# Other places in the SBUF partition for weights and activations of a 3-pass fp32 decoder trunk on one core

## The chip, the cores and the metric

The kernel runs on one NeuronCore of a Trainium2 chip. The metric is the device time of one execution in microseconds; 1004.0 us is the median of the two runs of the kernel before.

## The reference

Two decoder layers work on x of 256 tokens by 1024 features, all in float32. Layer 0 is a SwiGLU feed-forward (inner width 2816, added at half weight), a chunked gMLP mixer (inner width 2048) and a second feed-forward. Layer 1 is a feed-forward, stick-breaking attention (16 query heads on 4 key/value heads) and a feed-forward. Keys and values come from x between the two layers. Every sublayer reads an RMSNorm of x, and a last RMSNorm follows.

```python
def swiglu(h, w_in, w_out):
    gate, up = jnp.split(h @ w_in, 2, axis=-1)
    return (jax.nn.silu(gate) * up) @ w_out
...
x = x + 0.5 * swiglu(rms_norm(x, ffn_norm[i, 0]), ffn_w_in[i, 0], ffn_w_out[i, 0])
h = rms_norm(x, mix_norm[i])
x = x + (chunked_sgu(h, ...) if i < 1 else stick_breaking_attention(h @ b_w_q, k, v) @ b_w_o)
x = x + 0.5 * swiglu(rms_norm(x, ffn_norm[i, 1]), ffn_w_in[i, 1], ffn_w_out[i, 1])
```

## The kernel before, in words

Activations live transposed: features on the 128 partitions, 256 tokens along the partition. Each float32 operand is split into a high part, rounded to the matmul type fp32r, and a low part, the rest. One product is then three matmuls that add into one PSUM bank (`mm3`, lines 148 to 150):

```python
nc.tensor.matmul(o, al, bh, start=first, stop=False, skip_group_check=True)   # 148
nc.tensor.matmul(o, ah, bl, start=False, stop=False, skip_group_check=True)   # 149
nc.tensor.matmul(o, ah, bh, start=False, stop=last, skip_group_check=True)    # 150
```

The operand named second is streamed through the array, the one named first is loaded into it beforehand (the stationary one), by a weight load of 128 columns for each matmul. In the trace's names, `ga<-xnh,wlo` streams xnh and holds wlo.

**Weights** come in 332 units of 128 x 1024 floats. SyncE loads a unit into a `raw` tile (7 buffers, up to 7 units ahead), ScalarE casts it into `whi` (line 81), VectorE subtracts into `wlo` (line 83; 9 buffers each, up to 5 units ahead).

**The six stages that matter here**, in the order of the program, with the letters that the tile names end in:

- a, b, c, d are the four feed-forwards. The projection in (`ffn_in`, which calls `project`) holds weights and streams the activations xnh/xnl, 128 x 256 at a time, into the banks g and u: 11 steps of 96 matmuls. VectorE and ScalarE turn g and u into `hh`/`hl`. The projection out holds weights and streams hh/hl into the y banks (`Residual.add`), 11 steps of 48. In stage d the projection out is turned round (`out_add`): hh/hl is held, and 512 columns of weights are streamed into yo.
- s is the gMLP mixer: `project_rows` holds xnh/xnl and streams weights (bank v), `u_in` holds weights and streams xnh/xnl (bank uu), and the projection out streams hhs/hls (bank ys).
- q is the attention: the projection of q, then the steps z (q against the keys kz), o (weights a0, a1 against the values vd), and the projection out of oT (bank yo, streamed in 256 columns). Keys and values are made from xk just before stage c (banks kT and v).

All of these tiles come from pools which are laid one after the other along the partition, so a tile's byte address is settled by the sizes of what stands before it. In the built program xnh lies at byte 27,168 and xnl at 35,360 (both 32 modulo 128); the whi, wlo and raw buffers start at 75,872, 112,736 and 47,200 in steps of 4,096 (all 96 modulo 128); hh and hl start at 149,600 and 157,792 in steps of 2,048 (96); kz, vd, xk and oT lie at 0. Slices of them start at multiples of 512 bytes, so these remainders hold for every matmul. The instruction order is the program's own, engine by engine; pools set when a buffer is free again.

Of the kernel before, what the change touches and what calls it, by code (L numbers as in the profile page):

```python
# [8 lines left out]
F32 = mybir.dt.float32  # L9
F32R = mybir.dt.float32r  # L10
# [89 lines left out]
def trunk(  # L100
# [160 lines left out]
    xT = act.tile([P, KC, T], F32, name="xT")  # L261
    xnh = act.tile([P, KC, T], F32R, name="xnh")
    xnl = act.tile([P, KC, T], F32R, name="xnl")
    acc = act.tile([P, T], F32, name="acc")
    rT = act.tile([P, 2], F32, name="rT")

    spare = act.tile([P, P + 1 + 2 * (T + 1)], F32, name="spare")
    rb = spare[:, :T]
# [22 lines left out]

    eps = const.tile([P, 1], F32, name="eps")
    nc.vector.memset(eps, RMS_EPS)
# [38 lines left out]
    def load_x(hf):  # L332

        for d in range(hf * 4, hf * 4 + 4):
            ptr = ybank(f"ptr{d}")
            for tt in range(2):
                W.order(
                    nc.tensor.transpose(
                        ptr[:, tt * P : (tt + 1) * P], xin[tt, hf][:, (d % 4) * P : (d % 4 + 1) * P], ident
                    )  # L340
                )
            if d % 2:
                W.order(nc.vector.tensor_copy(xT[:, d, :], ptr[:, :T]))
            else:
                W.order(nc.scalar.copy(xT[:, d, :], ptr[:, :T]))
        for d in range(hf * 4, hf * 4 + 4):
            prepare(d, [(("ffn", 0), xnh, xnl)], False)
# [95 lines left out]

    XN = (xnh, xnl)

    def ffn_in(tag, j, ids, mid={}, by_bank=False):

        banks = [gbank(f"g{tag}_{j}"), gbank(f"u{tag}_{j}")]
        project(banks, ids, XN, mid, by_bank)
        gs = scratch(f"gs{tag}_{j}")  # L450
        us = scratch(f"us{tag}_{j}")
        nc.vector.tensor_mul(pair(gs), pair(banks[0]), bc2(rb))
        nc.scalar.activation(gs, gs, AF.Silu)
        nc.vector.tensor_mul(pair(us), pair(banks[1]), bc2(rb))
        nc.vector.tensor_mul(us, us, gs)
        hh = hp.tile([P, 512], F32R, tag="hh", name=f"hh{tag}_{j}")
        hl = hp.tile([P, 512], F32R, tag="hl", name=f"hl{tag}_{j}")
        split(hh, hl, us)
        return hh, hl
# [57 lines left out]
    def spatial_bias(hf):  # L517
# [16 lines left out]
        plan00,  # L534
        [(("mix", 0), xnh, xnl)],
        {1: lambda: load_x(1), 3: norm.columns, 4: norm.rows},
# [24 lines left out]
    norm = Rms("m0")  # L561
    project_rows(first[0], plan_v[0], XN, {2: norm.columns})
    project_rows(first[1], plan_v[1], XN, {2: norm.rows})
    for j in range(2):
        v_out(j, first[j])
    for j in range(2, 8):
        bank = gbank(f"v{j}")
        project_rows(bank, plan_v[j], XN)
        v_out(j, bank)
# [14 lines left out]
    def u_in(j):  # L584
        bank = gbank(f"uu{j}")
        project([bank], [[i] for i in plan_u["in", j]], XN)
        u = sg.tile([P, 512], F32, tag="u", name=f"usb{j}", bufs=4)
        nc.vector.tensor_mul(pair(u), pair(bank), bc2(rb))
        nc.scalar.activation(u, u, AF.Gelu_apprx_tanh)
        return u  # L590

    def mix(j, u):
# [20 lines left out]
        nc.vector.tensor_mul(s, s, u)  # L613
        hh = hp.tile([P, 512], F32R, tag="hh", name=f"hhs{j}")
        hl = hp.tile([P, 512], F32R, tag="hl", name=f"hls{j}")
        split(hh, hl, s)
# [6 lines left out]
    for kind, j in U_STEPS:  # L623
# [4 lines left out]
        else:  # L628
            h = hs.pop(j)
            for m in range(2):  # L630
# [3 lines left out]
                else:  # L634
                    tail.append((w, chunk(h, m)))
    close(y, tail, 0, 1.0, [(("ffn", 1), xnh, xnl)])
# [12 lines left out]
    norm = Rms("f1")  # L649
    ffn("b", plan01, [(("kv", 0), xkh, xkl), (("ffn", 2), xnh, xnl)], {1: norm.columns, 2: norm.rows})  # L650

# [24 lines left out]

    ffn("c", plan10, [(("mix", 1), xnh, xnl)])
    zscale = [at.tile([P, 2], F32, name=f"zscale{n}") for n in "pn"]
    oT = [at.tile([P, KC, T], F32R, tag=f"big{p}", name=f"oT{p}") for p in "hl"]

    def q_out(j, bank):
        qh = hp.tile([P, 512], F32R, tag="hh", name=f"qh{j}")
        ql = hp.tile([P, 512], F32R, tag="hl", name=f"ql{j}")
        split(qh, ql, bank)
        return qh, ql

    def q_in(j):
        bank = ybank(f"q{j}")
        project([bank], [[i] for i in plan_q[j]], XN)
        return q_out(j, bank)  # L690
# [58 lines left out]
    def values_of(b, a0, a1):  # L749
# [55 lines left out]
    close(y, tail, 0, 1.0, [(("ffn", 3), xnh, xnl)])  # L805
    att.close()
# [105 lines left out]
```

## Time and profile before

| | us |
|---|---|
| runs of the kernel before | 1003.92 and 1004.09, median 1004.0 |
| the profiled execution, its own time | 1004.4 |
| its span in the trace | 1002.7 |
| PE busy in the span | 982.3 (98%) |
| VectorE, ScalarE, GpSimd busy | 645.2, 504.1, 86.5 |

The span runs from the first to the last instruction; 1.7 us of the execution lie around it. A matmul's row gives the time at which it starts and a duration that runs on past the start of the next one, because matmuls are pipelined: the distance from one start to the next (called the pitch below) is what a matmul costs in a stream of them.

### The profile page before, as it was taken

How to read it: one execution, taken by the hardware profiler on the slowest of the kernel's cores; microseconds unless marked ns; L12 is line 12 of the kernel's file. 1: busy time of each engine (PE TensorE's matmuls, PEld its weight loads, DVE VectorE, ACT ScalarE, POOL GpSimd, SP SyncE). 2: the span in 40 equal slices, each digit the busy share in tenths (PEclk: the TensorE clock that was granted, in tenths of full speed). 3: DMA queues.
4: the chain of work that ended last, by engine and by line, in shares of the span. 5: the costliest groups of instructions: out<-in, count | busy, mean ns of one | idle time of the engine just before them, and what ended most of it. 6: DMA issues, size and time to landing. Idle time of an engine off the chain costs nothing.

```text
span 1002.7 us, 19306 instructions
## 1 busy us (share of the span) xinstructions
PE 982.3 (98%) x8042; PEld 963.5 (96%) x8042; DVE 645.2 (64%) x823; ACT 504.1 (50%) x690; POOL 86.5 (9%) x126
## 2 busy tenths in 40 slices
PE   8999999999999999999999999999997899999996
PEld 8999999999999999999999999999997899999996
DVE  6864675675866775656569755555678775565644
ACT  6643434475544564444448444444487674444433
POOL 4000000020000300000003000000046320000002
PEclk9999999999999999999999999999999999999999
DMA  9966565647555455666564866665643346656511
GB/s 304 322 195 190 169 189 188 190 143 222 184 177 175 133 191 188 193 188 193 186 195 146 247 189 191 189 193 186 190 149 92 97 147 191 207 172 203 176 42 43
DMA packets 135208, 179.56 MB, mean 179 GB/s; under 512 B 5624, under 2 KB 119376, under 8 KB 135120
## 3 DMA queue, kind: packets, MB, share of 16 engines
q1 hardware_dynamic: 134768, 177.76, 56.7%
q8 instruction: 63, 1.03, 0.4%
q0 software_dynamic: 192, 0.52, 0.2%
q14 instruction: 25, 0.20, 0.1%
q10 hardware_dynamic: 160, 0.05, 0.0%
HBM read 176.73 MB, written 1.05 MB: 177 GB/s over the span
## 4 chain that ended last, share of the span: by engine, by line
PE 89%; DVE 5%; ACT 2%; issue 1%; DMA 1%; POOL 1%; SPq 0%; ACTq 0%; POOLq 0%; DVEq 0%
PE yo L148 2%; PE yo L150 2%; PE yo L149 2%; PE yb L148 2%; PE yb L150 2%; PE yb L149 2%; PE ud L148 2%; PE ud L150 2%; PE gd L148 2%; PE ud L149 2%; PE gb L148 2%; PE gd L150 2%; PE gd L149 2%; PE ub L148 2%; PE gc L150 2%; PE gb L150 2%
## 5 line engine op out<-in xcount | busy, mean ns | idle before, releaser
L81 ACT CAST whi<-raw 128x1024 fp32r<-128x1024 f32 (+1 forms) x333 | 342.7, 1045 | 391.0 <-issue 205.3
L83 DVE TENSOR_TENSOR wlo<-raw,whi 128x1024 fp32r<-128x1024 f32 (+1 forms) x333 | 402.1, 1225 | 200.9 <-ACT whi L81 200.0
L290 POOL TENSOR_TENSOR acc<-acc,sq 128x256 f32<-128x256 f32 x39 | 33.8, 867 | 387.5 <-ACT sq L289 385.6
L148 PE MATMUL ga<-xnh,wlo 128*128 128x256 f32 x176 | 50.1, 285 | 0.0
L148 PE MATMUL ya<-hha,wlo 128*128 128x256 f32 x176 | 49.9, 284 | 0.2 <-DVE xT L399 0.2
L148 PE MATMUL yc<-hhc,wlo 128*128 128x256 f32 x176 | 49.9, 284 | 0.1
L148 PE MATMUL yb<-hhb,wlo 128*128 128x256 f32 x176 | 49.9, 284 | 0.0
L149 PE MATMUL ga<-xnl,whi 128*128 128x256 f32 x176 | 49.3, 280 | 0.5 <-DVE xnl L277 0.5
L149 PE MATMUL ya<-hla,whi 128*128 128x256 f32 x176 | 49.7, 282 | 0.0
L148 PE MATMUL gd<-xnh,wlo 128*128 128x256 f32 x176 | 49.7, 282 | 0.0
L149 PE MATMUL yb<-hlb,whi 128*128 128x256 f32 x176 | 49.7, 282 | 0.0
L149 PE MATMUL yc<-hlc,whi 128*128 128x256 f32 x176 | 49.7, 282 | 0.0
L150 PE MATMUL yb<-hhb,whi 128*128 128x256 f32 x176 | 49.6, 283 | 0.0
L148 PE MATMUL ua<-xnh,wlo 128*128 128x256 f32 x176 | 49.1, 279 | 0.5 <-DVE wlo L83 0.5
L150 PE MATMUL ya<-hha,whi 128*128 128x256 f32 x176 | 49.4, 283 | 0.0
L150 PE MATMUL gd<-xnh,whi 128*128 128x256 f32 x176 | 49.4, 281 | 0.0
L150 PE MATMUL ud<-xnh,whi 128*128 128x256 f32 x176 | 49.4, 281 | 0.0
L148 PE MATMUL ud<-xnh,wlo 128*128 128x256 f32 x176 | 49.4, 281 | 0.0
L149 PE MATMUL ud<-xnl,whi 128*128 128x256 f32 x176 | 49.4, 281 | 0.0
L149 PE MATMUL gd<-xnl,whi 128*128 128x256 f32 x176 | 49.4, 281 | 0.0
L150 PE MATMUL yc<-hhc,whi 128*128 128x256 f32 x176 | 49.4, 283 | 0.0
L150 PE MATMUL ga<-xnh,whi 128*128 128x256 f32 x176 | 49.1, 279 | 0.0
(289 smaller groups left out, 3353.6 us busy)
## 6 DMA issues: line engine op xcount, KB each, us to landing
raw<-in_ffn_w_in_dram SPq DMA_DIRECT2D x176, 512.0 KB, 4.5
raw<-in_ffn_w_out_dram SPq DMA_DIRECT2D x88, 512.0 KB, 4.3
raw<-in_a_w_in_dram SPq DMA_DIRECT2D x32, 512.0 KB, 4.4
raw<-in_a_w_out_dram SPq DMA_DIRECT2D x16, 512.0 KB, 3.3
raw<-in_b_w_q_dram SPq DMA_DIRECT2D x8, 512.0 KB, 4.5
raw<-in_b_w_o_dram SPq DMA_DIRECT2D x8, 512.0 KB, 4.0
raw<-in_w_kv_dram SPq DMA_DIRECT2D x4, 512.0 KB, 4.0
xin<-in_x_dram SPq DMA_DIRECT2D x4, 256.0 KB, 4.9
```

The costliest lines, as they stand in the source:

```text
L81: ins = nc.scalar.copy(hi[:, cc], raw[:, cc])
L83: ins = nc.vector.tensor_sub(lo[:, cc], raw[:, cc], hi[:, cc].bitcast(F32))
L148: nc.tensor.matmul(o, al, bh, start=first, stop=False, skip_group_check=True)
L149: nc.tensor.matmul(o, ah, bl, start=False, stop=False, skip_group_check=True)
L150: nc.tensor.matmul(o, ah, bh, start=False, stop=last, skip_group_check=True)
L290: nc.gpsimd.tensor_add(acc, acc, s)
```

## The change

No instruction is added, taken away or moved: on each of the five engines the order, the shapes and the waits are those of before. Only byte addresses change, through empty tiles (`gap`), padding, and wider tiles of which a shifted part is used. The scratch for dynamic DMA at the start of the partition shrinks from 16,384 to 8,192 bytes.

```diff
+    def gap(name, size):
+        pool = ctx.enter_context(tc.tile_pool(name=name, bufs=1))
+        pool.tile([P, size // 4], F32, name=f"{name}t")
...
+    gap("gapw", 32)
     rawp = ctx.enter_context(tc.tile_pool(name="rawp", bufs=7))
     hip = ctx.enter_context(tc.tile_pool(name="hip", bufs=9))
     lop = ctx.enter_context(tc.tile_pool(name="lop", bufs=9))
+    gap("gaph", 64)
...
+    SHIFT = {'a': 4, 's': 8, 'b': 12, 'c': 20, 'q': 24, 'd': 28}
+    def hp_tile(dtype, tag, name):
+        tile = hp.tile([P, 512 + 32], dtype, tag=tag, name=name)
+        n = place[0]
+        return tile[:, n : n + 512]
...
-    xnh = act.tile([P, KC, T], F32R, name="xnh")
-    xnl = act.tile([P, KC, T], F32R, name="xnl")
+    xnb = [act.tile([P, KC * T + 32], F32R, name=f"xn{p}") for p in "hl"]
+    def placed(n):
+        return tuple(t[:, n : n + KC * T].rearrange("p (k t) -> p k t", k=KC) for t in xnb)
+    XS = {n: placed(s) for n, s in {'a': 4, 's': 8, 'b': 12, 'c': 20, 'q': 24, 'd': 28}.items()}
...
-        project(banks, ids, XN, mid, by_bank)
+        place[0] = SHIFT[tag]
+        project(banks, ids, XS[tag], mid, by_bank)
...
-        hh = hp.tile([P, 512], F32R, tag="hh", name=f"hh{tag}_{j}")
-        hl = hp.tile([P, 512], F32R, tag="hl", name=f"hl{tag}_{j}")
+        hh = hp_tile(F32R, tag="hh", name=f"hh{tag}_{j}")
+        hl = hp_tile(F32R, tag="hl", name=f"hl{tag}_{j}")
...
+    at.tile([P, 8], F32, name="gapk")
     kz = [at.tile([P, 4, 2, T], F32R, name=f"kz{p}") for p in "hl"]
     vd = [at.tile([P, 2, 4, 2, 64], F32R, name=f"vd{p}") for p in "hl"]
+    at.tile([P, 16], F32, name="gapx")
...
-    nc = _bacc.Bacc("TRN2", target_bir_lowering=False, num_devices=1)
+    nc = _bacc.Bacc("TRN2", target_bir_lowering=False, num_devices=1, dynamic_dma_scratch_size=8192)
```

A shift counts floats, so 4 is 16 bytes. In the built program whi, wlo and raw lie at 64 modulo 128, the wide xn and hp tiles at 0 plus the shift. The table gives the remainders modulo 128 of the streamed and the held operand, and their distance (streamed minus held, modulo 128), for each stage.

| stage, banks | before: streamed, held | distance | after: streamed, held | distance |
|---|---|---|---|---|
| a in (ga, ua), a out (ya) | 32, 96 and 96, 96 | 64 and 0 | 16, 64 | 80 |
| s: v | 96, 32 | 64 | 64, 32 | 32 |
| s: uu, ys | 32, 96 and 96, 96 | 64 and 0 | 32, 64 | 96 |
| b in (gb, ub), b out (yb) | 32, 96 and 96, 96 | 64 and 0 | 48, 64 | 112 |
| keys, values: kT, v | 0, 96 and 96, 0 | 32 and 96 | 0, 64 and 64, 0 | 64 |
| c in (gc, uc), c out (yc) | 32, 96 and 96, 96 | 64 and 0 | 80, 64 | 16 |
| q: projection | 32, 96 | 64 | 96, 64 | 32 |
| q: z; o with a0 | 0, 96; 96, 0 | 32; 96 | 64, 96; 96, 64 | 96; 32 |
| q: yo | 0, 96 | 32 | 0, 64 | 64 |
| d in (gd, ud) | 32, 96 | 64 | 112, 64 | 48 |
| d out (yo, 512 columns) | 96, 96 | 0 | 64, 112 | 80 |

## Rows read from the trace of the kernel before

**Rows 1.** The page: span, part 1 for PE, part 2's granted clock.
```profile
span 1002.7 us, 19306 instructions
...
PE 982.3 (98%) x8042; PEld 963.5 (96%) x8042; DVE 645.2 (64%) x823; ACT 504.1 (50%) x690; POOL 86.5 (9%) x126
...
PEclk9999999999999999999999999999999999999999
```

**Rows 2.** The page, part 4: the chain that ended last, by engine.
```profile
PE 89%; DVE 5%; ACT 2%; issue 1%; DMA 1%; POOL 1%; SPq 0%; ACTq 0%; POOLq 0%; DVEq 0%
```

**Rows 3.** PE's waits: who for whom, us in total, times, longest.
```profile
PE o L149 <- DVE a0l L154: 6.1, 3, 3.5
```

**Rows 4.** Timeline of PE from 692 us: first and 30th row (start, duration, instruction).
```profile
691.78 0.28 PE L148 MATMUL gc<-xnh,wlo 128*128 128x256 f32 x1
...
695.07 0.28 PE L150 MATMUL gc<-xnh,whi 128*128 128x256 f32 x1
```

**Rows 5.** Timeline of PE from 701.55 us: first and 28th row.
```profile
701.37 0.28 PE L148 MATMUL yc<-hhc,wlo 128*128 128x256 f32 x1
...
704.61 0.28 PE L148 MATMUL yc<-hhc,wlo 128*128 128x256 f32 x1
```

**Rows 6.** Timeline of PE from 840 us: first and 30th row.
```profile
839.78 0.28 PE L148 MATMUL gd<-xnh,wlo 128*128 128x256 f32 x1
...
843.20 0.28 PE L150 MATMUL ud<-xnh,whi 128*128 128x256 f32 x1
```

**Rows 7.** Groups of 689.7–699.8, 701.4–705.6, 839–848 us: count | busy us, mean ns | idle.
```profile
L148 PE MATMUL uc<-xnh,wlo 128*128 128x256 f32 x16 | 4.4, 276 | 0.0
...
L149 PE MATMUL yc<-hlc,whi 128*128 128x256 f32 x13 | 3.7, 283 | 0.0
...
L148 PE MATMUL ud<-xnh,wlo 128*128 128x256 f32 x14 | 3.9, 281 | 0.0
```

**Rows 8.** Groups of the whole run, PE, shapes apart: the moved stages.
```profile
L150 PE MATMUL yc<-hhc,whi 128*128 128x256 f32 x176 | 49.4, 283 | 0.0
...
L150 PE MATMUL gd<-xnh,whi 128*128 128x256 f32 x176 | 49.4, 281 | 0.0
...
L150 PE MATMUL ga<-xnh,whi 128*128 128x256 f32 x176 | 49.1, 279 | 0.0
...
L150 PE MATMUL gb<-xnh,whi 128*128 128x256 f32 x176 | 48.7, 277 | 0.0
...
L150 PE MATMUL uc<-xnh,whi 128*128 128x256 f32 x176 | 48.6, 276 | 0.0
...
L149 PE MATMUL ys<-hls,whi 128*128 128x256 f32 x128 | 36.2, 283 | 0.0
...
L149 PE MATMUL v<-wlo,xnh 128*128 128x256 f32 x128 | 35.7, 279 | 0.0
L150 PE MATMUL uu<-xnh,whi 128*128 128x256 f32 x128 | 35.7, 279 | 0.0
...
L149 PE MATMUL yo<-wlo,hhd 128*128 128x512 f32 x82 | 31.9, 389 | 0.0
```

**Rows 9.** The same view: pairs at distances 32 and 96.
```profile
L150 PE MATMUL yo<-oTh,whi 128*128 128x256 f32 x64 | 17.8, 280 | 0.0
...
L149 PE MATMUL v<-wlo,xkh 128*128 128x256 f32 x16 | 4.5, 282 | 0.0
...
L149 PE MATMUL z<-kzl,qh 128*128 128x512 f32 x8 | 3.2, 397 | 0.0
```

**Rows 10.** Busy us (instructions) by engine in stage b: PE, PEld, DVE, ACT, POOL; PEclk.
```profile
345.00:535.00 190.00, 190.00 (x1636) 189.77 (x1635) 118.51 (x147) 92.89 (x124) 9.14 (x12) 1.00 0.59 183
```

**Rows 11.** DMA issues of the keys: KB, us to landing; the first use of kzh.
```profile
kzh<-kzh POOLq DMA_DIRECT2D x2, 128.0 KB, 5.5
...
L666 POOL DMA_DIRECT2D kzh<-kzh x2: 597/680/762, 547.8 to 548.6; - x2
...
L148 PEld LDWEIGHTS z<-kzh,ql x16: 187/188/192, 740.2 to 783.5; 128*128 128x128 f32 x16
```

More of the change, by code (lines that the diff above doesn't have):

```diff
@@ L134, in trunk @@
     py = ctx.enter_context(tc.tile_pool(name="py", bufs=4, space=PSUM))
+    place = [4]
+    SHIFT = {'a': 4, 's': 8, 'b': 12, 'c': 20, 'q': 24, 'd': 28}
     def gbank(name):
@@ L261, in trunk @@
     xT = act.tile([P, KC, T], F32, name="xT")
-    xnh = act.tile([P, KC, T], F32R, name="xnh")
-    xnl = act.tile([P, KC, T], F32R, name="xnl")
+    xnb = [act.tile([P, KC * T + 32], F32R, name=f"xn{p}") for p in "hl"]
+    def placed(n):
+        return tuple(t[:, n : n + KC * T].rearrange("p (k t) -> p k t", k=KC) for t in xnb)
+    XS = {n: placed(s) for n, s in {'a': 4, 's': 8, 'b': 12, 'c': 20, 'q': 24, 'd': 28}.items()}
     acc = act.tile([P, T], F32, name="acc")
     rT = act.tile([P, 2], F32, name="rT")
-    spare = act.tile([P, P + 1 + 2 * (T + 1)], F32, name="spare")
+    spare = act.tile([P, P + 1 + 2 * (T + 1)], F32, name="spare", padded_shape=[P, 672])
     rb = spare[:, :T]
@@ L290, in square @@
             nc.gpsimd.tensor_add(acc, acc, s)
-    eps = const.tile([P, 1], F32, name="eps")
+    eps = const.tile([P, 1], F32, name="eps", padded_shape=[P, 32])
     nc.vector.memset(eps, RMS_EPS)
@@ L346, in load_x @@
         for d in range(hf * 4, hf * 4 + 4):
-            prepare(d, [(("ffn", 0), xnh, xnl)], False)
+            prepare(d, [(("ffn", 0), *XS["a"])], False)
             if d % 2 == 0:
@@ L442, in project_rows @@
                 mid[kh + 1]()
-    XN = (xnh, xnl)
     def ffn_in(tag, j, ids, mid={}, by_bank=False):
         banks = [gbank(f"g{tag}_{j}"), gbank(f"u{tag}_{j}")]
-        project(banks, ids, XN, mid, by_bank)
+        place[0] = SHIFT[tag]
+        project(banks, ids, XS[tag], mid, by_bank)
         gs = scratch(f"gs{tag}_{j}")
@@ L534, in trunk @@
         plan00,
-        [(("mix", 0), xnh, xnl)],
+        [(("mix", 0), *XS["s"])],
         {1: lambda: load_x(1), 3: norm.columns, 4: norm.rows},
@@ L561, in trunk @@
     norm = Rms("m0")
-    project_rows(first[0], plan_v[0], XN, {2: norm.columns})
-    project_rows(first[1], plan_v[1], XN, {2: norm.rows})
+    project_rows(first[0], plan_v[0], XS["s"], {2: norm.columns})
+    project_rows(first[1], plan_v[1], XS["s"], {2: norm.rows})
     for j in range(2):
@@ L567, in trunk @@
         bank = gbank(f"v{j}")
-        project_rows(bank, plan_v[j], XN)
+        project_rows(bank, plan_v[j], XS["s"])
         v_out(j, bank)
@@ L585, in u_in @@
         bank = gbank(f"uu{j}")
-        project([bank], [[i] for i in plan_u["in", j]], XN)
+        project([bank], [[i] for i in plan_u["in", j]], XS["s"])
+        place[0] = SHIFT["s"]
         u = sg.tile([P, 512], F32, tag="u", name=f"usb{j}", bufs=4)
@@ L613, in mix @@
         nc.vector.tensor_mul(s, s, u)
-        hh = hp.tile([P, 512], F32R, tag="hh", name=f"hhs{j}")
-        hl = hp.tile([P, 512], F32R, tag="hl", name=f"hls{j}")
+        hh = hp_tile(F32R, tag="hh", name=f"hhs{j}")
+        hl = hp_tile(F32R, tag="hl", name=f"hls{j}")
         split(hh, hl, s)
@@ L635, in trunk @@
                     tail.append((w, chunk(h, m)))
-    close(y, tail, 0, 1.0, [(("ffn", 1), xnh, xnl)])
+    close(y, tail, 0, 1.0, [(("ffn", 1), *XS["b"])])
     sgu.close()
@@ L649, in trunk @@
     norm = Rms("f1")
-    ffn("b", plan01, [(("kv", 0), xkh, xkl), (("ffn", 2), xnh, xnl)], {1: norm.columns, 2: norm.rows})
+    ffn("b", plan01, [(("kv", 0), xkh, xkl), (("ffn", 2), *XS["c"])], {1: norm.columns, 2: norm.rows})
     XK = (xkh, xkl)
@@ L675, in trunk @@
             split(vd[0][:, tt, :, r, :], vd[1][:, tt, :, r, :], src)
-    ffn("c", plan10, [(("mix", 1), xnh, xnl)])
+    ffn("c", plan10, [(("mix", 1), *XS["q"])])
     zscale = [at.tile([P, 2], F32, name=f"zscale{n}") for n in "pn"]
@@ L681, in q_out @@
     def q_out(j, bank):
-        qh = hp.tile([P, 512], F32R, tag="hh", name=f"qh{j}")
-        ql = hp.tile([P, 512], F32R, tag="hl", name=f"ql{j}")
+        qh = hp_tile(F32R, tag="hh", name=f"qh{j}")
+        ql = hp_tile(F32R, tag="hl", name=f"ql{j}")
         split(qh, ql, bank)
@@ L688, in q_in @@
         bank = ybank(f"q{j}")
-        project([bank], [[i] for i in plan_q[j]], XN)
+        project([bank], [[i] for i in plan_q[j]], XS["q"])
         return q_out(j, bank)
@@ L742, in transposed @@
             nc.tensor.transpose(t1[:, h * P : (h + 1) * P], a[1][:, h, P:], ident)
-        a0 = [hp.tile([P, 512], F32R, tag=f"h{p}", name=f"a0{p}{b}") for p in "hl"]
+        a0 = [hp_tile(F32R, tag=f"h{p}", name=f"a0{p}{b}") for p in "hl"]
         a1 = [hp.tile([P, T], F32R, tag=f"a1{p}", name=f"a1{p}{b}", bufs=2) for p in "hl"]
@@ L764, in values_of @@
         split(oT[0][:, b, :], oT[1][:, b, :], of)
+    place[0] = SHIFT["q"]
     qs, es, aw, at2 = {}, {}, {}, {}
@@ L768, in trunk @@
     first = [ybank(f"q{j}") for j in range(2)]
-    project([first[0]], [[i] for i in plan_q[0]], XN, {2: norm.columns})
-    project([first[1]], [[i] for i in plan_q[1]], XN)
+    project([first[0]], [[i] for i in plan_q[0]], XS["q"], {2: norm.columns})
+    project([first[1]], [[i] for i in plan_q[1]], XS["q"])
     for t, s in zip(zscale, (0.125, -0.125)):
@@ L804, in trunk @@
             att_step(step[0], int(step[1]))
-    close(y, tail, 0, 1.0, [(("ffn", 3), xnh, xnl)])
+    close(y, tail, 0, 1.0, [(("ffn", 3), *XS["d"])])
     att.close()
```

## The prediction

> **What bounds the kernel now.** I read the page's parts 1 and 2 first. PE is busy for 982.3 of 1002.7 us, and the granted clock is full in all 40 slices [rows 1], so neither a slower clock nor idle time explains much. The chain that ended last is PE for 89% [rows 2], and the longest wait of PE for another engine is 6.1 us in total, in the attention [rows 3]. So the time is the number of matmuls times their pitch, and a change of places can only matter through the pitch.
>
> The pitch is read from the timeline. In stage c's projection in, 29 pitches take 695.07 − 691.78 = 3.29 us, which is 113.4 ns each [rows 4]. In the projection out that follows, 27 pitches take 704.61 − 701.37 = 3.24 us, 120.0 ns each [rows 5]. In stage d's projection in, 29 pitches take 843.20 − 839.78 = 3.42 us, 117.9 ns each [rows 6]. Shape, type and clock are the same in all three. The mean durations in the three stretches are 276, 283 and 281 ns [rows 7]; less the pitch, each leaves 163 ns. That gives a ruler for the gapless groups: pitch = mean duration − 163.
>
> With it the whole run reads as follows [rows 8]: a's projection in 116 ns, b's 114, c's 113, d's 118, the mixer's uu and v 116, the projections out 120, and the turned projection out of d 226 ns for 512 columns. What differs between in and out is the distance of streamed and held operand modulo 128: 64 in, 0 out. But place does not settle it alone: c and d have the same places and run at 113 and 118, and a lies between. So distance 64 allows two pitches, which one stage holds for long stretches, and distance 0 gives 120 and nothing else for long. Pairs at other distances are rare: the attention's yo at distance 32 runs at 280 − 163 = 117, the values' v at 96 at 282 − 163 = 119, and z (512 columns, distance 32) at 397 − 163 = 234 against 226 at distance 0 [rows 9].
>
> **The change part by part.** Since no instruction, order or wait changes, each part is a count times a change of pitch. Nothing in the trace shows 16, 48, 80 or 112 as a distance. The bounds are the fastest and the slowest steady pitch of the 256-column rows, 113.4 and 120 ns [rows 4, 5]. Both signs are open: a moved pair may fall into the fast rhythm or into the slow one. I take 117.5 for every moved pair, which lies between the 117 of yo at distance 32 and the slow rhythm of distance 64 at 117.9 [rows 6, 9]; nothing picks one new distance over another, and these are the rows where a pair holds neither extreme. Each feed-forward has 6 groups of 176 matmuls in (1056) and 3 of 176 out (528).
>
> - b in: 1056 × (117.5 − 114) = +3.7 us. The distance goes from 64 to 112, so the fast rhythm goes, as far as I can tell.
> - c in: 1056 × (117.5 − 113.4) = +4.3 us.
> - a in: 1056 × (117.5 − 116) = +1.6 us. d in: 1056 × (117.5 − 118) = −0.5 us.
> - uu, 384 matmuls: +1.5 ns each, +0.6 us. v, 384: the same, +0.6 us.
> - a, b and c out: 1584 × (117.5 − 120) = −4.0 us. ys, 384: −1.0 us. Distance 0 goes everywhere, and 120 with it.
> - d out, 246 matmuls of 512 columns: between the 226 of distance 0 and the 234 of z [rows 8, 9] I take 229, nearer to the row that has this stage's own shape and operands; 246 × 2.5 = +0.6 us.
> - yo of the attention, 192 matmuls, from distance 32 to 64: from 117 to 115.5, the middle of the two pitches of distance 64, −0.3 us.
> - The other pairs of the attention and of keys and values are some 350 matmuls; 3 ns on each would be 1 us, and I leave them at 0.
>
> The sum is +5.6 us, against the profiled execution of 1004.4 us, which stands 0.4 us above the median. On the median that is 1004.0 + 5.6, or 1010.
>
> What else moves with the addresses: VectorE, ScalarE and the DMAs write and read at the new places. In stage b VectorE is busy for 118.51 and ScalarE for 92.89 of 190 us [rows 10], so a third of VectorE's time covers any slower access, up to about 70 us in that stage; above that the weight split of line 83 would come late. With PE faster by 6% at the very most, that cover stays. The smaller DMA scratch serves the DMAs that GpSimd issues; the key copies are such, they land 5.5 us after issue, near 554 us, and PE first loads against kzh at 740.2 us [rows 11]. I cost both at nothing, and they would have to be late by nearly 190 us to cost anything.
>
> **The rivals.**
>
> *All moved pairs fall into the fast rhythm.* In its favour, it is the state in which stages b and c spend most of their time [rows 8], and 113.4 is what a pair reaches when nothing holds it up as far as this trace goes. Against it, none of the pairs at distance 0, 32 or 96 reaches it in the mean, and even distance 64 lost it through the whole of d. Its sum: b −0.6, a −2.7, d −4.9, uu −1.0, v −1.0, the three outs 1584 × −6.6 = −10.5, ys −2.5, d out 246 × −6.6 = −1.6, yo −0.7: −26 us, 978 us.
>
> *The new distances lock at the slow rhythm.* Distance 0 held 120 ns for thousands of matmuls, so a slow rhythm is as stable as the fast one, and v at distance 96 stands at 119 [rows 9]. If every moved pair goes to 120, the projections in pay: b +6.3, c +7.0, a +4.2, d +2.1, uu +1.5, v +1.5, and d out at 234 pays +2.0, yo +0.6, while the outs gain nothing: +25 us, 1029 us. A matmul of 256 columns counts about 7,000 times among the moved pairs, so 1 ns is 7 us. From a mean moved pitch of 119.6 ns on, 2.1 ns above my 117.5, the result is slower by over 2% (20 us), which is about what a measurement of this kernel can tell from no change.
>
> *The places do nothing.* The difference between in and out could come from something other than the place, such as the pattern of PSUM banks. Then every group keeps its pitch, and the time stays at 1004 us. Against it: v streams weights and holds activations, with the places of uu exchanged, and has the pitch of uu, not that of the outs [rows 8]; and z and yo differ from the outs in the direction in which their distances differ [rows 9]. For it: c and d differ at equal places. The Trainium skill, in "SBUF — State Buffer", section "Who interferes with whom", gives PE two independent read ports, one for the streamed operand and one for weight loads, and says that PE never waits for anyone. By that rule no place could cost anything and the sum would be 0; the trace with 113.4 and 120.0 ns for one shape at one clock does not bear it out so far, so this rival keeps a small chance.
>
> **How the numbers follow.** My forecast, a mixture of rhythms about 117.5 ns with stages of both signs, gets 0.70; the fast lock 0.06; the slow lock 0.12; no effect 0.12. Of the six new distances some will lie above 117.5 and some below; if each stage of some 1,500 matmuls is off by 2.5 ns either way, that is 4 us a stage, and about 9 us for six independent ones. The range goes from 990 to 1028, two such steps to either side and rounded outward below, so that it takes in most of the slow lock and leaves out the outer part of the fast one. Faster by over 2% is the fast lock alone, 0.06; slower is the slow lock, 0.12; within 2% is all the rest, 0.82.
>
> **What would show it right or wrong.** The order of instructions stays, so each group of rows 8 can be laid beside its own successor. If I am right, the groups of ya, yb, yc and ys fall from 283 towards 280 ns, those of b and c in rise from 277 and 276 towards 280, and d in stays near 281. Different distances should give different pitches; if all groups stand unchanged, the places do nothing. A stage at a mean of 276 or 283 throughout has locked fast or slow. I would be wrong in kind, not in size, if PE's waits for VectorE or for DMA grew from a few us to tens, if the granted clock fell, or if a group went clearly above 283 or below 276, outside both bounds.

## The result and the profile after

The changed kernel takes 1014.84 us (median of 1014.15 and 1015.53), the kernel before 1004.0. The ratio is 1.0109, 95% interval 1.008 to 1.0139: slower by about 1%. The profiled execution took 1015.53 us.

The page of the changed kernel: span, part 1 for PE, the granted clock, and part 4 by engine.
```profile
span 1013.8 us, 19306 instructions
...
PE 996.1 (98%) x8042; PEld 976.9 (96%) x8042; DVE 643.3 (63%) x823; ACT 503.7 (50%) x690; POOL 85.0 (8%) x126
...
PEclk9999999999999999999999999999999999999999
...
PE 89%; DVE 5%; ACT 2%; issue 1%; POOL 1%; DMA 1%; SPq 0%; ACTq 0%; POOLq 0%; DVEq 0%
```

PE's waits in the changed kernel (us in total, times, longest), the two largest.
```profile
PE o L166 <- DVE a0l L171: 4.6, 2, 3.4
PE o L165 <- DVE a0l L171: 2.4, 1, 2.4
```

The span grew by 11.1 us and PE's busy time by 996.1 − 982.3 = 13.8 us, with the same 8,042 matmuls at the same full clock [rows 1]. The chain is PE for 89% as before [rows 2], the waits in the attention stay at a few us (4.6 + 2.4 in total; the largest total before was 6.1 [rows 3]), and PE's idle time in the span went from 1002.7 − 982.3 = 20.4 to 17.7 us. So the time is not in waits; the matmuls follow one another more slowly. One stretch of stage b shows it: the columns are those of rows 10, PE's instructions stand in its first bracket.
```profile
345.00:535.00 190.00, 190.00 (x1617) 189.69 (x1616) 116.41 (x141) 90.09 (x115) 5.83 (x9) 1.00 0.60 186
```
In the same 190 us without a gap, 1,617 matmuls start where 1,636 did [rows 10]. VectorE and ScalarE have as much room as before.

Groups of the whole run in the changed kernel, shapes apart (count | busy us, mean ns of one | idle); lines 165 to 167 are 148 to 150 of before.
```profile
L167 PE MATMUL gb<-xnh,whi 128*128 128x256 f32 x176 | 50.0, 284 | 0.0
...
L167 PE MATMUL ya<-hha,whi 128*128 128x256 f32 x176 | 49.3, 282 | 0.0
...
L167 PE MATMUL uc<-xnh,whi 128*128 128x256 f32 x176 | 49.3, 280 | 0.0
...
L166 PE MATMUL gb<-xnl,whi 128*128 128x256 f32 x176 | 49.2, 279 | 0.0
...
L167 PE MATMUL gd<-xnh,whi 128*128 128x256 f32 x176 | 49.1, 279 | 0.0
...
L167 PE MATMUL yc<-hhc,whi 128*128 128x256 f32 x176 | 49.0, 280 | 0.0
...
L165 PE MATMUL gb<-xnh,wlo 128*128 128x256 f32 x176 | 49.0, 278 | 0.0
...
L167 PE MATMUL yb<-hhb,whi 128*128 128x256 f32 x176 | 48.6, 277 | 0.0
...
L167 PE MATMUL uu<-xnh,whi 128*128 128x256 f32 x128 | 36.1, 282 | 0.0
...
L166 PE MATMUL v<-wlo,xnh 128*128 128x256 f32 x128 | 36.0, 281 | 0.0
L166 PE MATMUL ys<-hls,whi 128*128 128x256 f32 x128 | 36.0, 281 | 0.0
...
L166 PE MATMUL yo<-wlo,hhd 128*128 128x512 f32 x82 | 32.3, 394 | 0.0
```
Each line against its own successor in rows 8: b and c in rise from 277 and 276 to 284 and 280, uu and v from 279 to 282 and 281, and d out from 389 to 394; d in falls from 281 to 279. The outs part: b falls from 283 to 277, c to 280, ys to 281, a only to 282. The three lines of one product no longer agree (b in: 278, 279 and 284), so a single group's mean is not a measure of its stage here.

From here on the pitch is the mean distance from one start to the next over a whole stage, worked out from the starts in each trace (distances over 150 ns left out, over 270 ns for d out). By it, after minus before is, in us: a in 1056 × 2.8 ns = 2.9, b in 1056 × 4.1 = 4.3, c in 1056 × 4.3 = 4.5, d in 0.2, uu 1.2, v 0.2, a out −0.1, b out −2.2, c out −0.5, ys −0.3, d out 246 × 4.8 = 1.2, q 0.4. The sum is 11.8 us, for 11.1 in the span. So the pitches account for the whole difference.

The most telling rows are in b out, which streams hh and hl from one of four buffers in turn. First and last of the 48 matmuls of four steps, one after the other, in the timeline of the changed kernel:
```profile
391.14 0.28 PE L165 MATMUL yb<-hhb,wlo 128*128 128x256 f32 x1
...
396.46 0.28 PE L167 MATMUL yb<-hhb,whi 128*128 128x256 f32 x1
...
407.88 0.28 PE L165 MATMUL yb<-hhb,wlo 128*128 128x256 f32 x1
...
413.39 0.28 PE L167 MATMUL yb<-hhb,whi 128*128 128x256 f32 x1
...
424.82 0.28 PE L165 MATMUL yb<-hhb,wlo 128*128 128x256 f32 x1
...
430.15 0.28 PE L167 MATMUL yb<-hhb,whi 128*128 128x256 f32 x1
...
441.57 0.28 PE L165 MATMUL yb<-hhb,wlo 128*128 128x256 f32 x1
...
447.08 0.28 PE L167 MATMUL yb<-hhb,whi 128*128 128x256 f32 x1
```
47 pitches take 5.32, 5.51, 5.33 and 5.51 us: 113.2, 117.2, 113.4, 117.2 ns (the rows are rounded to 0.01 us, so a pitch read off two of them is good to some 0.2 ns over 47 matmuls and 0.6 ns over 16). The pitch alternates with the buffer. All four buffers are at 48 modulo 128; but the widened tile is 2,176 bytes, 8.5 × 256, so in the built program they lie at 176 and 48 modulo 256 in turn. The same happens to the widened xn: 8,320 bytes are 32.5 × 256, so xnh and xnl lie on different halves of 256 bytes, and each product of three matmuls streams from both.

### The profile page after: what moved, and what is told of

The parts are those of the page before. It is cut to its first block, busy times and chain, and to the rows that moved or that the text cites. A ratio compares the mean times of both kernels' runs of the same rounds, so it can differ in the third digit from the quotient of the medians.

```text
span 1013.8 us, 19306 instructions
## 1 busy us (share of the span) xinstructions
PE 996.1 (98%) x8042; PEld 976.9 (96%) x8042; DVE 643.3 (63%) x823; ACT 503.7 (50%) x690; POOL 85.0 (8%) x126
## 4 chain that ended last, share of the span: by engine, by line
PE 89%; DVE 5%; ACT 2%; issue 1%; POOL 1%; DMA 1%; SPq 0%; ACTq 0%; POOLq 0%; DVEq 0%
PE yo L165 2%; PE yo L167 2%; PE yo L166 2%; PE ub L167 2%; PE gb L167 2%; PE gc L166 2%; PE uc L166 2%; PE gb L166 2%; PE gc L165 2%; PE ub L166 2%; PE uc L165 2%; PE uc L167 2%; PE ud L165 2%; PE gc L167 2%; PE gd L165 2%; PE ud L166 2%
## 5 line engine op out<-in xcount | busy, mean ns | idle before, releaser
L167 PE MATMUL gb<-xnh,whi 128*128 128x256 f32 x176 | 50.0, 284 | 0.0
L167 PE MATMUL ub<-xnh,whi 128*128 128x256 f32 x176 | 50.0, 284 | 0.0
L166 PE MATMUL gc<-xnl,whi 128*128 128x256 f32 x176 | 49.6, 282 | 0.0
L166 PE MATMUL uc<-xnl,whi 128*128 128x256 f32 x176 | 49.6, 282 | 0.0
L165 PE MATMUL gc<-xnh,wlo 128*128 128x256 f32 x176 | 49.5, 281 | 0.0
L167 PE MATMUL ua<-xnh,whi 128*128 128x256 f32 x176 | 49.4, 281 | 0.0
L165 PE MATMUL uc<-xnh,wlo 128*128 128x256 f32 x176 | 49.3, 280 | 0.0
```

## The experiments

Twelve runs. The table holds the pitch in ns of each stage for all of them, worked out from the starts as above (d out: 512 columns). "Held" in v and in d out is the activation, elsewhere the weight.

| kernel | a in | a out | v | uu | ys | b in | b out | c in | c out | d in | d out |
|---|---|---|---|---|---|---|---|---|---|---|---|
| before | 115.1 | 119.7 | 117.2 | 115.3 | 119.8 | 114.1 | 119.6 | 113.5 | 119.6 | 117.6 | 227.1 |
| after | 117.9 | 119.5 | 117.9 | 118.5 | 119.0 | 118.2 | 115.5 | 117.8 | 118.7 | 117.8 | 231.9 |
| e1_all64 | 117.7 | 116.0 | 113.7 | 117.6 | 116.0 | 117.5 | 115.8 | 117.5 | 116.0 | 117.5 | 231.9 |
| e2_in64 | 117.7 | 118.6 | 113.7 | 117.7 | 119.0 | 117.5 | 116.0 | 117.8 | 116.5 | 117.5 | 231.9 |
| e3_out0 | 117.9 | 119.2 | 117.9 | 118.5 | 119.3 | 118.3 | 119.3 | 117.8 | 119.7 | 117.8 | 230.5 |
| e4_scratch | 115.0 | 119.6 | 117.2 | 115.3 | 119.7 | 114.1 | 119.6 | 113.5 | 119.6 | 117.7 | 227.1 |
| e5_all0 | 114.0 | 114.0 | 117.2 | 115.7 | 114.5 | 117.8 | 117.6 | 117.8 | 117.8 | 117.7 | 229.7 |
| e12_all0_again | 115.1 | 115.2 | 117.2 | 116.6 | 114.7 | 117.8 | 117.6 | 117.8 | 117.6 | 114.2 | 229.0 |
| e6_all128 | 117.8 | 117.8 | 114.0 | 116.1 | 117.1 | 117.8 | 117.7 | 117.8 | 117.8 | 117.8 | 233.3 |
| e7_same256 | 119.1 | 119.1 | 116.7 | 118.3 | 118.3 | 117.2 | 117.2 | 118.7 | 118.7 | 118.4 | 233.3 |
| e8_same256up | 119.2 | 119.2 | 117.7 | 119.9 | 119.9 | 113.4 | 113.6 | 118.7 | 118.6 | 119.2 | 230.0 |
| e9_all176 | 113.7 | 113.6 | 120.0 | 113.7 | 114.9 | 113.4 | 113.6 | 113.4 | 113.6 | 113.8 | 228.1 |
| e10_v208 | 113.7 | 113.6 | 120.0 | 118.6 | 115.0 | 113.4 | 113.7 | 113.4 | 113.5 | 114.0 | 233.3 |
| e11_all112 | 113.8 | 113.6 | 120.1 | 113.7 | 114.8 | 113.4 | 113.6 | 113.4 | 113.6 | 113.9 | 228.1 |

### One part at a time: e1_all64, e2_in64, e3_out0, e4_scratch

The theory was that of the prediction: the distance of streamed and held operand modulo 128 sets the pitch. **e1** puts every stage at distance 64, by shifts of 0.
```diff
-    SHIFT = {'a': 4, 's': 8, 'b': 12, 'c': 20, 'q': 24, 'd': 28}
+    SHIFT = {'a': 0, 's': 0, 'b': 0, 'c': 0, 'q': 0, 'd': 0}
-    XS = {n: placed(s) for n, s in {'a': 4, 's': 8, 'b': 12, 'c': 20, 'q': 24, 'd': 28}.items()}
+    XS = {n: placed(s) for n, s in {'a': 0, 's': 0, 'b': 0, 'c': 0, 'q': 0, 'd': 0}.items()}
```


> All shifts 0: activations and hh/hl at 0 and weights at 64 modulo 128, so that the streamed and the held operand stand 64 apart in every stage, in and out. Place theory (the distance modulo 128 sets which pitches are open to a pair): every group takes the two pitches of distance 64 that the kernel before shows, 113.3 and 117.8 ns; the projections out fall from 120 to between these, the projections in stay as in the kernel before; 991 to 1000 us. Rival, the position in the instruction stream (in against out) sets the pitch: the outs stay near 120, about 1004 us. Rival, it is the smaller DMA scratch or the gaps: 1010 us or more.

Measured: 1008.3 us, ratio 1.0043 (1.0028 to 1.0058), against 991 to 1000 by the theory. Not borne out; and neither rival had this time (about 1004; 1010 or more). Groups of e1:
```profile
L167 PE MATMUL gc<-xnh,whi 128*128 128x256 f32 x176 | 49.5, 281 | 0.0
...
L167 PE MATMUL yb<-hhb,whi 128*128 128x256 f32 x176 | 48.8, 278 | 0.0
```
The ins of c have the distance of before and yet 281 ns where there were 276 [rows 8], 117.5 as a pitch. The outs, at that distance too, average 116, which refutes the rival that had them near 120; taken buffer by buffer they are 113.9 in a when the buffer lies at 0 modulo 256 and 117.7 at 128.

**e2** has the activations of the ins at shift 0 and leaves the rest of the change (only the line of XS above).

> Of the change, the places of xnh/xnl alone undone: they stand 64 from the weights again, while hh/hl keep the six new places. Place theory: the projections in go back to the pitches of the kernel before (a 116, b 114, c 113.4, d 118, uu 116 ns), the outs keep those of the changed kernel (ya 119.5, yb 115.5, yc 118.7, yo 232); about 1002 us. Rival, the rhythm is handed on from the stretch before, so that an out in another rhythm drags the next in along: ins near 118 ns, 1010 us or more.

Measured: 1010.36 us, ratio 1.007 (1.0053 to 1.0086). Not borne out either: the ins stay at 117.5 to 117.8 although their distance modulo 128 is back. What is not back is the width of the tiles. The numbers are those of the rival, a rhythm handed on from the outs (ins near 118, 1010 us or more); e3 tests it the other way round. One out moved with no edit of its own: c went from 118.7 to 116.5, because its buffers at 80 modulo 256 ran at 113.9 here and at 118.7 in the changed kernel.

**e3** moves hh and hl of a, s, b, c and d to 64, so that the outs are at distance 0 modulo 128 again (modulo 256, half of the buffers lie at 64 and half at 192).
```diff
-    SHIFT = {'a': 4, 's': 8, 'b': 12, 'c': 20, 'q': 24, 'd': 28}
+    SHIFT = {'a': 16, 's': 16, 'b': 16, 'c': 16, 'q': 24, 'd': 16}
```


> Of the change, the places of hh/hl alone undone: they stand at the weights' own place again (distance 0), q keeps its place, xnh/xnl keep the six new ones. Place theory: outs back at 120 ns and yo at 227, the ins as in the changed kernel, near 118; about 1017 us. Rival, the handed-on rhythm: ins return toward the kernel before, under 1010 us.

Measured: 1016.77 us, ratio 1.0129 (1.0113 to 1.0144), as expected, and the outs of b go from 115.5 to 119.3. The ins stay at 117.8 to 118.5 with the outs back at 119.2 to 119.7, against the rival of a handed-on rhythm, which had them return and the time under 1010 us. d out missed: 230.5, not 227, as its buffers at 192 run at 233.3. So the change's outs are worth about 2 us together, and its ins carry the loss.

**e4** is the kernel before with the smaller scratch alone, which moves every tile down by 8,192 bytes.
```diff
-    nc = _bacc.Bacc("TRN2", target_bir_lowering=False, num_devices=1)
+    nc = _bacc.Bacc("TRN2", target_bir_lowering=False, num_devices=1, dynamic_dma_scratch_size=8192)
```


> The kernel before with the 8 KB scratch alone; all addresses fall by 8,192 bytes, so every remainder modulo 128 and every distance stays. Place theory: 1004 us, within 0.3%. Rival, the scratch or the absolute address matters: 1008 us or more.

Measured: 1003.9 us, ratio 0.9999 (0.999 to 1.0008), with the pitches of before in each column. The scratch and the common base do nothing.

### Remainders modulo 256: e5_all0, e6_all128, e7_same256, e8_same256up

The theory of the distance modulo 128 had fallen, and the alternation from buffer to buffer led to the next: the pitch goes by the two places modulo 256. All kernels from here on start from the changed kernel with tiles of whole multiples of 256 bytes, so that high and low and all buffers agree; weights lie at 64 modulo 256 (whi, wlo, raw).
```diff
-    gap("gapw", 32)
+    gap("gapw", 160)
-    gap("gaph", 64)
+    gap("gaph", 192)
-        tile = hp.tile([P, 512 + 32], dtype, tag=tag, name=name)
+        tile = hp.tile([P, 512 + 64], dtype, tag=tag, name=name)
+    act.tile([P, 32], F32, name="gapn")
-    xnb = [act.tile([P, KC * T + 32], F32R, name=f"xn{p}") for p in "hl"]
+    xnb = [act.tile([P, KC * T + 64], F32R, name=f"xn{p}") for p in "hl"]
```
They differ in the two tables of shifts (SHIFT and XS, equal): e5 0 everywhere, e6 32 floats (128 bytes) everywhere, e7 the change's own, e8 the change's own plus 32 floats.

> Tile steps of xn and hp are widened to whole multiples of 256 bytes, so the high and low tiles and all buffers of one operand share a remainder modulo 256. Streamed activations lie at 0 and weights at 64 modulo 256 in every stage. Theory (the pitch goes by the two remainders modulo 256): in the run with everything at distance 64 modulo 128, the outs that streamed from 0 with weights at 64 ran at 113.8 ns, so ins and outs both run at 113.3 to 114 ns, groups of 276 to 277 ns mean, and the kernel at 983 to 987 us. Rival (only the distance modulo 128 counts, and each stage enters one of two rhythms by its history): as in that run, ins 117.5, outs 116, 1008 us.

> The same kernel with the activations at 128 instead of 0 modulo 256, weights still at 64: the distance modulo 128 is unchanged. Theory (remainders modulo 256): the outs that streamed from 128 with weights at 64 ran at 117.7 ns, so ins and outs run at 117 to 118 ns, groups of 280 to 281 ns mean, and the kernel at 1008 to 1013 us, over 20 us slower than the one with activations at 0. Rival (distance modulo 128 only): equal to the one with activations at 0 within 3 us.

> The change's own shifts of 16, 32, 48, 80, 96 and 112 bytes, but high and low tiles and all buffers at that remainder modulo 256, weights at 64. Theory (remainders modulo 256): ins and outs of a stage run alike, at the pitch that the outs of the changed kernel showed at the same remainders: a (16) 118 to 119, mixer (32) 118, b (48) 117.2, c (80) 113.8 or 118.7; about 1008 to 1014 us with c slow, 1000 to 1007 with c fast. Rival (the high and the low tile lying on different halves is what slows the ins of the changed kernel): ins fall to 113 to 115 ns in most stages, under 1000 us.

> The same with 128 bytes added to every activation (144, 160, 176, 208, 224, 240 modulo 256). Theory (remainders modulo 256): a (144) 120.0 in and out, mixer (160) 119.9, b (176) 113.4 in and out, c (208) 118.7: a in group near 283 ns, b in group near 276 ns. With q and d at 117 to 118 this is about 1008 to 1016 us. Rival (distance modulo 128 only): every stage as in the kernel without the 128 bytes, equal to it within 3 us, and b no faster than a.

Measured: e5 1002.79 us (ratio 0.9988, 0.9974 to 1.0003), e6 1011.32 (1.0067, 1.0052 to 1.0082), e7 1015.28 (1.0102, 1.0082 to 1.0123), e8 1013.19 (1.0088, 1.0071 to 1.0105).

e7 and e8 decide between a period of 128 and one of 256, by their stages: their times differ by 2.1 us, which the rival (equal within 3 us) allowed too. PE's timeline in stage b, first and 30th row from 400 us, in e7 (48 modulo 256) and then in e8 (176):
```profile
399.81 0.28 PE L167 MATMUL ub<-xnh,whi 128*128 128x256 f32 x1
...
403.21 0.28 PE L166 MATMUL gb<-xnl,whi 128*128 128x256 f32 x1
```
```profile
399.77 0.28 PE L165 MATMUL gb<-xnh,wlo 128*128 128x256 f32 x1
...
403.05 0.28 PE L167 MATMUL gb<-xnh,whi 128*128 128x256 f32 x1
```
29 pitches take 3.40 and 3.28 us, 117.2 and 113.1 ns, at the same distance modulo 128; over the whole stage 117.2 and 113.4. Ins and outs now agree within 0.3 ns in a, b and c of both kernels, so what part of the program a matmul stands in does not matter. Steps of 2,304 bytes put the hp buffers on alternate halves of 512 bytes, and b out is still at 113.6: a period of 512 is not needed. Two numbers missed: a at 144 was expected at 120 and has 119.2, and e7, with c slow, ended 1.3 us above its 1008 to 1014.

The same two kernels refute the rival that mixing halves is what slows all ins. Unmixed, a, c and d are slower (119.1, 118.7, 118.4) than mixed in the changed kernel (117.9, 117.8, 117.8); only b pays for the mixture, 118.2 against 117.2 and 113.4. A triple (the three matmuls of one product) that streams from both halves comes to 117.5 to 118.5 at every shift tried.

Nor is it the other engines that get in PE's way at the new places. In b in, by the starts, e8 took 113.4 ns a matmul in the 199 triples during which VectorE, ScalarE or GpSimd was at work and 113.3 in the 102 during which none was; e7 took 117.2 and 117.1. DMAs ran throughout and are not told apart by this.

e6 came out as expected in time and in the ins and outs of a to d (uu and ys, at 116.1 and 117.1, have fast stretches). e5 missed by 16 us: a in and out run at 114, but b, c and d at 117.7, a value that the outs of e1 had almost only on the other half. So e6 stands 8.5 us above e5, not over 20.

### Two rhythms at one pair of places: e12_all0_again

e5's runs spread over 8 us, from 999.6 to 1007.78. Its kernel was profiled once more, without any edit.

> The kernel with activations at 0 and weights at 64 once more, unchanged: its executions spread over 8 us (999.6 to 1007.8), those with 176 over 1.6 us. Theory (two rhythms are open at this pair, and small differences in an execution decide which one a stretch takes): in this second profile the mean pitch of at least one of the stages a to d in, or of uu, v or ys, differs by 1.5 ns or more from the first profile (a 114, b, c, d 118, uu 116, v 117, ys 114.5). Rival (the program and its places fix the rhythm, and the spread comes from elsewhere): every group within 1 ns of the first profile.

Measured: 1003.53 us. PE's timeline from 841.6 us in e5 and then in e12, both in stage d's projection in, 17 rows apart:
```profile
841.63 0.28 PE L165 MATMUL ud<-xnh,wlo 128*128 128x256 f32 x1
...
843.51 0.28 PE L166 MATMUL ud<-xnl,whi 128*128 128x256 f32 x1
```
```profile
841.68 0.28 PE L165 MATMUL ud<-xnh,wlo 128*128 128x256 f32 x1
...
843.49 0.28 PE L166 MATMUL ud<-xnl,whi 128*128 128x256 f32 x1
```
16 pitches take 1.88 and 1.81 us, 117.5 and 113.1 ns. The mean of d in is 117.7 in one execution and 114.2 in the other, of one and the same kernel: 1056 × 3.5 ns = 3.7 us that no place explains. In e12, 279 of 349 triples of d in take 113 ns each, 59 take 118, and few lie between. So the pair of 0 and 64 has two rhythms and can enter either. That is what before shows as well, with 32 and 96, in c (113.5) and d (117.6).

When the rhythm can change shows in stage a of e12: first and last of 27 matmuls of the out, the four small matmuls that interrupt, first and last of 27 matmuls of the in that follows.
```profile
106.28 0.28 PE L165 MATMUL ya<-hha,wlo 128*128 128x256 f32 x1
...
109.34 0.28 PE L167 MATMUL ya<-hha,whi 128*128 128x256 f32 x1
109.46 0.60 PE L537 MATMUL pws<-ident,wsbs 128*128 128x128 f32 x4
...
110.61 0.28 PE L165 MATMUL ua<-xnh,wlo 128*128 128x256 f32 x1
...
113.55 0.28 PE L167 MATMUL ua<-xnh,whi 128*128 128x256 f32 x1
```
26 pitches take 3.06 us before it and 2.94 after, 117.7 and 113.1 ns. Taken by triples (fast below 115.4 ns a matmul, slow from 116.4) over the ins of a to d, the outs of a to c, uu and ys, the rhythm changes 26 times in e5, 40 in e12 and 6 in e6. Each change comes within three triples of an interruption, that is, of a start-to-start distance of over 140 ns or of other matmuls in between; in an unbroken stream none does. So in these three kernels' runs a stretch kept its rhythm, fast or slow, until PE was interrupted. b and c in stood at 117.8 in both executions, so it is not chance alone that picks it.

### A pair that returns to the fast rhythm: e9_all176, e10_v208, e11_all112

176 with 64 was fast throughout b in e8. **e9** puts every stage there (shift 44 floats), and hh and hl of d, which are held, at 64.
```diff
-    SHIFT = {'a': 4, 's': 8, 'b': 12, 'c': 20, 'q': 24, 'd': 28}
+    SHIFT = {'a': 44, 's': 44, 'b': 44, 'c': 44, 'q': 44, 'd': 16}
-    XS = {n: placed(s) for n, s in {'a': 4, 's': 8, 'b': 12, 'c': 20, 'q': 24, 'd': 28}.items()}
+    XS = {n: placed(s) for n, s in {'a': 44, 's': 44, 'b': 44, 'c': 44, 'q': 44, 'd': 44}.items()}
```


> Activations at 176 modulo 256 in every stage, weights at 64; in stage d hh and hl, held there, at 64 too. Theory (the pitch goes by the places modulo 256, and 176 with 64 has only the fast rhythm): 113.4 to 113.6 ns in and out in all of a, b, c, d, uu and ys, groups of 276 to 277 ns mean; d out 227 to 228. Against the kernel with 128 added to the change's places (1013.2 us): a in and out 1584 x 5.8 ns = 9.2 us, c the same by 5.2 = 8.3, d in 1056 x 5.8 = 6.1, uu and ys 768 x 6.6 = 5.1, q and d out 1.3, 30 us in all: 983 to 986 us. Rival (two rhythms at every place, the choice made by what stage b met in that run): some stages fast and some at 118, 990 to 1006 us.

**e10** differs from e9 in two entries, **e11** in lying 64 bytes lower with weights, activations and d's hp tiles.
```diff
-    SHIFT = {'a': 44, 's': 44, 'b': 44, 'c': 44, 'q': 44, 'd': 16}
+    SHIFT = {'a': 44, 's': 44, 'b': 44, 'c': 44, 'q': 44, 'd': 52}
-    XS = {n: placed(s) for n, s in {'a': 44, 's': 44, 'b': 44, 'c': 44, 'q': 44, 'd': 44}.items()}
+    XS = {n: placed(s) for n, s in {'a': 44, 's': 52, 'b': 44, 'c': 44, 'q': 44, 'd': 44}.items()}
```
```diff
-    gap("gapw", 160)
+    gap("gapw", 96)
-    gap("gaph", 192)
+    gap("gaph", 256)
-    SHIFT = {'a': 44, 's': 44, 'b': 44, 'c': 44, 'q': 44, 'd': 16}
+    SHIFT = {'a': 28, 's': 28, 'b': 28, 'c': 28, 'q': 28, 'd': 0}
-    XS = {n: placed(s) for n, s in {'a': 44, 's': 44, 'b': 44, 'c': 44, 'q': 44, 'd': 44}.items()}
+    XS = {n: placed(s) for n, s in {'a': 28, 's': 28, 'b': 28, 'c': 28, 'q': 28, 'd': 28}.items()}
```


> As the kernel with 176 everywhere, but the mixer's xnh and xnl at 208, and hh and hl of stage d at 208. Theory: uu, which streams from 208, goes from 113.4 to 118.7 ns (+2.0 us). If only the distance streamed minus held modulo 256 counts, v, which streams from 64 and holds 208, is at the distance 112 of the fast pair and runs at 113.4; if the two places count each for itself, it runs at 116 to 119. d out, 512 columns streamed from 64 with 208 held, goes to 227 by the distance, to 230 to 233 otherwise. The rest stays as in the kernel with 176 everywhere; time within 3 us of it.

> The kernel with 176 everywhere, but all of these places 64 bytes lower: activations at 112, weights at 0, hh and hl of stage d at 0 modulo 256. The distance streamed minus held is still 112. If only the distance modulo 256 counts: equal to the kernel with 176 everywhere within 3 us, 983 to 988. If the absolute places count: some other pitch, between 113.4 and 120 ns in all stages alike, 990 to 1025 us.

Measured: e9 986.79 us, ratio 0.9831 (0.9814 to 0.9847); e10 990.89 us, 0.9868 (0.9854 to 0.9883); e11 988.1 us, 0.9843 (0.9828 to 0.9858). e9 beats both kernels, by 1.7% and, medians against each other, 986.79 / 1014.84, by 2.8%. Page and groups of e9:
```profile
PE 966.1 (98%) x8042; PEld 946.7 (96%) x8042; DVE 642.4 (65%) x823; ACT 504.2 (51%) x690; POOL 86.5 (9%) x126
...
L166 PE MATMUL gc<-xnl,whi 128*128 128x256 f32 x176 | 48.4, 275 | 0.0
L167 PE MATMUL yc<-hhc,whi 128*128 128x256 f32 x176 | 48.1, 275 | 0.0
...
L166 PE MATMUL v<-wlo,xnh 128*128 128x256 f32 x128 | 36.3, 283 | 0.0
```
In and out of c are at 275 ns, one ns below the fastest group of before [rows 8], and b, c and their outs hold 113.4 to 113.6 over the whole stage. e9 stands 0.8 us above its range: v, which I had not priced, rose to 120.0, and ys and d in keep some slow stretches (114.9, 113.8).

The pair is not free of a slower pace: 102 triples of e9 in the same stages take 116.4 ns a matmul or more. But by the starts all of these in e9, e10 and e11 are among the first five after an interruption, and the rest of the stretch is fast. In e5 and e12 some 1,300 slow triples each are the tenth or a later one. That is the difference between this pair and that of 0 and 64.

e10 stands 4.1 us above e9, where at most 3 was expected. e10 and e11 ask what a pair is. Groups of e10, then of e11:
```profile
L166 PE MATMUL v<-wlo,xnh 128*128 128x256 f32 x128 | 36.2, 283 | 0.0
...
L167 PE MATMUL uu<-xnh,whi 128*128 128x256 f32 x128 | 36.0, 281 | 0.0
```
```profile
L166 PE MATMUL gb<-xnl,whi 128*128 128x256 f32 x176 | 48.4, 275 | 0.0
...
L166 PE MATMUL v<-wlo,xnh 128*128 128x256 f32 x128 | 36.3, 283 | 0.0
```
In e11 both places move by 64 bytes and every column of the table stays within 0.2 ns, the fast ones and the slow v alike. The held place counts as well as the streamed one: d in streams from 112 in e7 and in e11 and has 118.4 with weights at 64 and 113.9 with weights at 0. In e10, uu goes to 118.6 as expected; but v, which streams from 64 and holds 208, is at the distance 112 of the fast pair (176 − 64) and has 120.0, above both forecasts (113.4 by the distance, 116 to 119 otherwise). So if v may be set beside the ins, the distance modulo 256 alone does not decide: a common move of 64 bytes leaves the pitch, a common move by 112 does not. For it speaks that v agrees with the q projection at two other distances (116.7 and 116.9 in e7, both 117.7 in e8). But v is the only long stage of 256 columns that holds activations, so role and stage are not told apart. d out has 233.3 and not the 227 expected, which settles nothing here: 227 had been measured at distance 0 and no 512-column pair at 112 elsewhere.

## Why the prediction came out as it did

The forecast of 1010 was 4.8 us low, the sign was right and the range held. What a place costs, and why, was not: the bracket about 117.5 held for the ins by luck, as the last point says. By its own steps:

- **What bounds the kernel** held: same instructions, clock, chain and waits, and the whole difference in the pitch. Vector and scalar work and the scratch cost nothing, as the step said (e4 for the scratch).
- **b, c, uu in** were right in mechanism as far as it went: the fast rhythm went. At 118.2, 117.8 and 118.5 in place of 117.5 they paid 4.3, 4.5 and 1.2 us for 3.7, 4.3 and 0.6. **a in** paid 2.9 for 1.6; most of the difference is the ruler, which had put before at 116 where its starts give 115.1: 1056 × 0.9 ns = 1.0 us. The same ruler had put yo at 117, where the starts give 118.1, so distance 32 was not below the slow rhythm of distance 64. **d in** rose by 0.2 us where −0.5 was forecast, and **v** by 0.2 us for 0.6. The 284 of gb lies above the 283 that was named as a bound; it is one line of a mixed triple, and the stage's pitch, 118.2, is within.
- **The outs** are the step that failed: "Distance 0 goes everywhere, and 120 with it." Leaving distance 0 does not take the slow pitch away. The outs were to give 5.0 us with ys and gave 3.1: b 2.2, c 0.5, a 0.1, ys 0.3. Other places are nearly as slow: 16, 32, 80, 144, 160 and 208 run at 118 to 120 in e7 and e8, with weights at 64 modulo 256. Of b's 2.2 us some 1.6 come from the two of its four buffers that happened to lie at 176 (264 × 6.2 ns), 0.6 from those at 48.
- **d out** was sized from its neighbours at 229, which is up 3 ns from 226, though the sum took 2.5; by the starts it went from 227.1 to 231.9, up 4.8, 1.2 us for 0.6.
- **Why a place costs** was wrong. The prediction took the distance modulo 128 as the key, and the shifts as six new distances. e7 against e8 shows 128 bytes to matter (b 117.2 and 113.4). And the change's ins do not show six distances at all: with their halves mixed they stand at 117.8 to 118.5, and at shift 0 at nearly the same (117.5 to 117.8 in e1 and e2). That 117.5 was nearly right for them is thus luck of the middle.

Of the rivals, that *places do nothing* is refuted, by e9 above all: 17 us by addresses alone. The Trainium skill, in "SBUF — State Buffer", section "Who interferes with whom", has PE's two read ports independent and PE waiting for nobody. Read as the prediction read it, no column of the table could move by that, and they move between 113.4 and 120.1 ns at a full clock. The *slow lock* (1029 us, just outside the range that was to take in most of it) did not come; nearest to it are the mixer of e8 at 119.9 and v in e9 at 120.0, and no kernel has it in all stages. The *fast rhythm for all* had been put at 978 us, 26 below before; the change does not reach it, but e9, by other places, has 17 of the 26. The reason given against it, that even distance 64 lost it for the whole of d, mistook a pair with two rhythms for the best there is.

By the starts, the gain of e9 over before is: outs 528 × (6.1 + 6.0 + 6.0) = 9.6 us, d in 1056 × 3.8 = 4.0, a in 1.5, ys 1.9, b in 0.8, uu 0.6, less 1.1 in v: 17.3 of the 18.0 us between the spans. The larger part is the outs, at the distance 0 that the change rightly left.

Open stays what in the chip makes the pitch depend on the places, which of the two rhythms a stretch enters after an interruption, whether 0 and 128 differ with weights at 64 (uu is at 116.1 in e6, with 43 of 126 triples fast), whether v is slow by its role or its stage, and which common moves are neutral. Moves by 32 and 96 seem so too: distance 0 runs at 119.6 to 119.9 at 96 and 96 (before), 64 and 64 (e3) and 0 and 0 (the keys and values of e11), and 32 with 96 has the two rhythms of 0 with 64.

## What to carry to other kernels

When PE is busy without a gap at a full clock, lay the start-to-start distances of equal matmuls side by side, buffer by buffer: 113 against 120 ns is 6%, and only addresses may differ. Look at streamed and held operand modulo 256, and give tiles a size that is a multiple of 256, or buffers of one pool will differ among themselves. Do not choose a pair by a mean, nor by one stage: a mean of 115 or 116 can be two rhythms, and a pair with two can hold one of them over a whole stage, as before does in c, and take the other in the next stage or the next execution. Put the pair into every stage, as e9 does, and see whether it comes back to the fast rhythm after an interruption.

## What the runs showed of the hardware that was not expected

- At full clock one shape (256 columns, 128 x 128 held) has steady pitches from 113.4 to 120.1 ns, by the bytes at which its operands lie modulo 256.
- At 0 with 64 modulo 256 there are two rhythms, 113.3 and 117.8 ns, and one kernel took either in the same stage in two executions (d in, 117.7 and 114.2). Either rhythm lasted until PE was interrupted. The ten runs of e5 spread over 8 us, the four of e9 over 1.6 us; but before, whose pair has two rhythms as well, spreads over only 3.4 us in the 13 runs taken beside e5. 80 with 64 has a second one as well: in c out the buffer at 80 ran at 113.9 in e2 and c at 118.7 in e7.
- Three matmuls that stream from both halves of 256 bytes in turn come to 117.5 to 118.5 ns at every shift tried, even where each half alone gives 117.2 and 113.4 (b).
- Moving both operands by 64 bytes changes nothing (e9, e11: within 0.2 ns in every stage); v with 64 streamed and 208 held, at the same distance, has 120.0 where the ins with 176 streamed and 64 held have 113.4.
- d out, 512 columns, ranges from 227.1 ns (96 and 96) over 228.1 (64 and 64) to 233.3 (64 with 112, 128 or 208 held). Distance 0, the slowest for 256 columns, is the fastest for 512.
